# Seven block products for eight over eighteen down-projection blocks in two stages, with p1 first

## The chip, the cores and the metric

The kernel runs on one core of one Trainium2 chip. The metric is device time in microseconds (us) of one execution. The kernel before takes 1212.17 us, the median of three runs (1211.62 to 1212.28).

## The reference, cut to what matters

Two layers (`DEPTH` 2) on 512 tokens (`S`) of width 1024. Each layer is an attention part (retention and stick-breaking heads sharing one input and one output projection) and a SwiGLU feed-forward part with an inner width of 2816, all in float32:

```
h = rms_norm(x, norm2_g[l])
x = x + (jax.nn.silu(h @ w_gate[l]) * (h @ w_up[l])) @ w_down[l]
```

The change touches only the product with `w_down`. The inner width is 22 blocks of 128. For two of these blocks, an even and an odd one, the product is a sum of 2 by 2 blocks: two token halves of 256, two inner blocks of 128, two output halves of 512. Such a product can be had with seven block products in place of eight, from sums and differences of the blocks (Strassen's scheme).

## The kernel before, in words

Every float32 operand is split into a high and a low part, and each product is three matmuls: high by high, high by low, low by high (`mm3`). The high part is a cast on ScalarE (ACT), the low part a subtraction on VectorE (DVE). TensorE (PE) runs its matmuls in the order in which the program is written; the instructions of the other engines are put in order ahead of time by a scheduler, which orders them by priority and estimated time. Each engine, and the queue of loads on SyncE (SP), then works in that order.

Weights come as a stream (`WeightStream`): units of 1024 columns are loaded by SP into four raw buffers, and split by ACT (`whi`) and DVE (`wlo`) into three buffers. A unit is used by 24 matmuls of 512 columns; the split of a unit goes into the buffer of the one three places ahead of it, once PE is done with that.

The feed-forward part of a layer (`ffn`) runs on PE as follows. For each of the 22 blocks f: a gate product and an up product of 24 matmuls each, into two banks out of three (`acc`). DVE multiplies both by the token scale (`g`, `u`), ACT applies silu, DVE multiplies `u` by `g`. For f below 10 (`HALVES[0]`), `paired` then forms what the seven products need of the activations: `a11`, and, when the odd block is there, the split of `u` and of two tiles of differences (the tiles `f`, split into `fhi` and `flo`). `f75` serves the products r7 and q5, `f63` serves q6 and q3. At f=4, 5 and 6 the blocks of `w_down` are asked for (`load_pair`, L732 to L735, tiles `q`, 256 KB each), and DVE adds the first two of each pair (L735); the scheduler is free to put loads and sums earlier.

After f=9 comes the stage of seven products (`down_seven`), for five pairs: q5, p1, q3, q6, r7, p2, q4, each a sum over the five pairs into one group of PSUM banks. The `w_down` operands of the products are made by DVE from the loaded blocks (`summed`), and split like the weights. In layer 0 a pair takes 7 x 4 x 3 = 84 matmuls of 256 columns, where the plain product takes 2 x 8 x 3 = 48 matmuls of 512 columns. In layer 1 a pair takes 7 x 2 x 3 = 42 matmuls of 512 columns. The results are added to the residual by DVE; q5, p1 and q6 are copied by ACT first.

Then gate and up of f=10 to 21, with the activations split into `ahi` and `alo`, and the rest: the plain product with `w_down` over these twelve blocks, 288 matmuls in each layer. In layer 0 it goes by output blocks d (8 of them); after each, DVE adds the bank to `x[d]`, and `feed` prepares the next layer's input: `hhi` (ACT), `hlo` (DVE), the square (ACT) and the sum of squares `ssq` (GpSimd, POOL). In layer 1 it goes by token blocks, and the final norm follows.

Of the kernel before, what the change touches and what calls it, by code (L numbers as in the profile page):

```python
# [18 lines left out]
P = 128  # L19
DM = 1024  # L20
S = 512
L = 2
# [5 lines left out]
FT = DFF // P  # L28
# [24 lines left out]

SEVEN = ("q5", "p1", "q3", "q6", "r7", "p2", "q4")
PAIRS = 5
HALVES = range(2 * PAIRS), range(2 * PAIRS, FT)
TH = S // 2

SLOTS = 26
# [5 lines left out]
def block_plan():  # L67

    plan = []

    def cols(name, l, col):
        return [(name, l, k, col, P) for k in range(KT)]

    for l in range(L):
        plan += [("w_in", l, k, SV, 512) for k in range(KT)]
        for h in range(NH):
            for c in (SQ, SK, RG):
                plan += cols("w_in", l, c + h * HD)
        plan += [("w_in", l, k, RV, 512) for k in range(KT)]
        for h in range(NH):  # L80
            plan += cols("w_in", l, RQ + h * HD) + cols("w_in", l, RK + h * HD)
        for ds, ks in OUT:
            plan += [("w_out", l, k, d * P, P) for d in ds for k in ks]
        for k in range(KT):
            for f in range(2):
                plan += [("w_gate", l, k, f * P, P), ("w_up", l, k, f * P, P)]
        for half, fs in enumerate(HALVES):
            for f in fs:
                if f >= 2:
                    plan += cols("w_gate", l, f * P) + cols("w_up", l, f * P)  # L90
            if half == 0:
                plan += [("seven", l, p, i, 512) for p in SEVEN for i in range(PAIRS)]
            elif l < L - 1:
                for d in range(KT):
                    plan += [("w_down", l, f, d * P, P) for f in fs]
            else:
                for dh in range(2):
                    plan += [("w_down", l, f, dh * 512, 512) for f in fs]
    return plan
# [138 lines left out]
def layers(ctx, tc, xg_in, xT_in, ws_in, wd_in, gfin_in, cos_in, sin_in, dec_in, out):  # L238
    nc = tc.nc
# [9 lines left out]
    pe = Stream(nc)  # L249
    wst = WeightStream(nc, wpool, rawpool, ws_in)  # L250
# [29 lines left out]
    for k in range(KT):  # L280
# [23 lines left out]
        out=mask16, in_=mask16, compare_op=ALU.is_gt, fill=-BIG,  # L304
# [405 lines left out]
    def ffn(l):  # L710
        last = l == L - 1
        with tc.tile_pool(name=f"ff{l}", bufs=1, reuse_waits="tile") as sb:
# [11 lines left out]

            b11, b12, b22, b21 = {}, {}, {}, {}

            def load_block(to, i, n, odd, dh):
                to[i] = block(n)
                nc.sync.dma_start(out=to[i], in_=wd_in[l, 2 * i + odd, :, dh * 512 : dh * 512 + 512])

            def load_pair(i):
                load_block(b12, i, i, 0, 1)  # L732
                load_block(b11, i, PAIRS + i, 0, 0)
                load_block(b22, i, 2 * PAIRS + i, 1, 1)
                nc.vector.tensor_tensor(out=b12[i], in0=b12[i], in1=b11[i], op=ALU.add)  # L735

            def summed(p, i):

                if p == "q6":
                    nc.vector.tensor_tensor(out=b12[i], in0=b12[i], in1=b22[i], op=ALU.add)  # L740
                    load_block(b21, i, 2 * PAIRS + i, 1, 0)
                elif p == "r7":
                    nc.vector.tensor_tensor(out=b11[i], in0=b12[i], in1=b11[i], op=ALU.subtract)
                elif p == "q4":
                    nc.vector.tensor_tensor(out=b12[i], in0=b12[i], in1=b21[i], op=ALU.add)
                src = {"p1": b11, "r7": b11, "p2": b21, "q3": b22}.get(p, b12)
                return src[i]
# [37 lines left out]
            def gated(f, pg, pu):  # L785
                g = sb.tile([P, S], F32, tag="g", name="g", bufs=2)
                nc.vector.tensor_tensor(out=g, in0=pg, in1=rs, op=ALU.mult)  # L787
                act(out=g, in_=g, func=AF.Silu)
                u = sb.tile([P, S], F32, tag="u", name="u", bufs=3)
                nc.vector.tensor_tensor(out=u, in0=pu, in1=rs, op=ALU.mult)  # L790
                nc.vector.tensor_tensor(out=u, in0=u, in1=g, op=ALU.mult)  # L791
                if f in HALVES[0]:
                    return paired(f, u)
                n = 2 * (f - HALVES[1][0])
                hi, lo = slot(n, "ahi"), slot(n + 1, "alo")
                split(hi, lo, u)
                acts[f] = hi, lo

            even, fac = {}, {p: [] for p in SEVEN}
            t0, t1 = slice(0, TH), slice(TH, S)  # L800

            def paired(f, u):


                def home(n, name):
                    n += f // 2 * 7
                    if n < SLOTS:
                        return slot(n, name)
                    return sb.tile([P, S], F32R, tag=f"more{n}", name=name, bufs=1)

                def both(n, src, p, q):
                    hi, lo = home(n, "fhi"), home(n + 1, "flo")
                    split(hi, lo, src)
                    fac[p].append((hi[:, t0], lo[:, t0]))
                    fac[q].append((hi[:, t1], lo[:, t1]))

                def minus(out, a, b):
                    nc.vector.tensor_tensor(out=out, in0=a, in1=b, op=ALU.subtract)
# [12 lines left out]
                both(0, f75, "r7", "q5")  # L831
                minus(f63[:, t0], v[:, t0], f75[:, t1])
                minus(f63[:, t1], u[:, t0], f63[:, t0])
                both(2, f63, "q6", "q3")

            def down_seven():
                n = 2 if last else 4
                w = 512 if last else TH

                def part(t, dh, j):  # L840
                    if last:
                        return xtd[2 * t + j][:, dh * 512 : dh * 512 + 512]
                    return x[4 * dh + j][:, t * TH : t * TH + TH]
# [2 lines left out]

                def evac(p, ps, j):
                    def put(t, dh, op):
                        y = part(t, dh, j)
# [19 lines left out]

                for m, p in enumerate(SEVEN):  # L870
                    if last:
                        pss = [bank() if m % 3 == 2 else bank("z", 4) for _ in range(n)]
                    else:
                        pss = banks_b() if m % 2 else banks_a()
                    for i in range(PAIRS):
                        b = wst.block("seven", l, p, i, 512)
                        a = fac[p][i]
                        for j in range(n):
                            c = slice(j * P, j * P + P)
                            if last:  # L880
                                pe.mm3(pss[j], [v[:, c] for v in a], b, i == 0, i == PAIRS - 1)
                            else:
                                pe.mm3(
                                    pss[j][:, :TH], [v[:, c] for v in b], a,
                                    i == 0, i == PAIRS - 1,
                                )
                    for j in range(n):
                        evac(p, pss[j][:, :w], j)

                def to(t, dh, j, src, op=ALU.add):  # L890
                    y = part(t, dh, j)
# [24 lines left out]
                for tb in range(TB):  # L916
                    pe.later(8000 + 4000 * tb, lambda tb=tb: turn(tb))

            for half, fs in enumerate(HALVES):
                if half == 1 and last:  # L920
                    gfin = [block(KT + i) for i in range(2)]
                    for dh in range(2):
                        nc.sync.dma_start(out=gfin[dh], in_=gfin_in[:, dh * 512 : dh * 512 + 512])
                for f in fs:
                    if f < 2:
                        continue
                    for i in {4: (0, 1), 5: (2, 3), 6: (4,)}.get(f, ()):
                        load_pair(i)
                    pg, pu = bank(), bank()
                    for ps, name in ((pg, "w_gate"), (pu, "w_up")):  # L930
                        for k in range(KT):
                            w = wst.block(name, l, k, f * P, P)
                            pe.mm3(ps, w, (hhi[k], hlo[k]), k == 0, k == KT - 1)
                    gated(f, pg, pu)
                if half == 0:
                    down_seven()
                    continue
                if not last:
                    table_set(EXP_LN)
# [97 lines left out]
```

## Time and profile before

| | |
|---|---|
| median of three runs | 1212.17 us |
| the profiled execution | 1213.44 us |
| its span | 1211.7 us |
| PE busy | 1197.0 us (99%) |
| DVE busy | 750.4 us (62%) |
| ACT busy | 533.4 us (44%) |
| POOL busy | 149.3 us (12%) |

The span is the time from the first to the last record of the profile; the execution is 1.74 us longer. A busy share is an average over all stages; the view by stretches shows the stages apart. The time of a matmul in the records (about 0.39 us for 512 columns) overlaps with the next one's, so the pace of PE is read from the distance between starts.

### The profile page before, as it was taken

Reading aid. Unit: us, or ns where it says so; the run is one execution under the profiler, and the core shown is the slowest. Engines: PE = TensorE matmul, PEld = TensorE weight load, DVE = VectorE, ACT = ScalarE, POOL = GpSimd, SP = SyncE. Lnnn points to the kernel's source line nnn. Section 1 sums busy time; section 2 is a strip of 40 time slices with the busy share of each in tenths; the row PEclk is TensorE's granted clock in tenths of the full one; section 3 lists DMA queues with packets and bytes.
Section 4 is the critical chain, followed back from the end, with each engine's and each line's share of the span. In section 5 each row is a group of like instructions: output and inputs, shape, how many; then the busy total and the mean of one; then the engine's idle time right before and its main releaser. Section 6 shows DMA issues by size and latency. Waiting matters only on the chain.

```text
span 1211.7 us, 14527 instructions
## 1 busy us (share of the span) xinstructions
PE 1197.0 (99%) x5624; PEld 995.5 (82%) x5624; DVE 750.4 (62%) x1048; ACT 533.4 (44%) x812; POOL 149.3 (12%) x135
## 2 busy tenths in 40 slices
PE   9999999999999999999999999999999999999997
PEld 7888887878889988888888888878888788888886
DVE  7566788696568744444344668887865785444333
ACT  6467645453335332333334766444533442332323
POOL 1122054030000000001112212432200000000011
PEclk9999999999999999999999999999999999999999
DMA  7322222353211233233332222224342113232321
GB/s 261 105 70 70 87 89 70 102 202 97 94 53 44 70 105 96 95 99 110 104 105 87 70 70 85 90 70 140 115 139 102 35 62 104 87 104 89 103 70 70
DMA packets 36790, 115.79 MB, mean 96 GB/s; under 512 B 4081, under 2 KB 4081, under 8 KB 36721
## 3 DMA queue, kind: packets, MB, share of 16 engines
q1 hardware_dynamic: 36576, 114.60, 28.1%
q8 instruction: 44, 0.72, 0.2%
q10 hardware_dynamic: 144, 0.26, 0.1%
q14 instruction: 26, 0.20, 0.1%
HBM read 112.75 MB, written 2.10 MB: 95 GB/s over the span
## 4 chain that ended last, share of the span: by engine, by line
PE 91%; DVE 4%; POOL 2%; issue 1%; ACT 1%; DMA 1%; SPq 0%; POOLq 0%; ACTq 0%; DVEq 0%
PE acc L217 69%; PE z L217 17%; PE o L217 4%; PE z L228 1%; POOL k L475 1%; POOL slo L326 1%; POOL qlo L326 1%; DVE wlo L159 0%; ACT whi L157 0%; DMA q<-wd 0%; POOL q L475 0%; DVE p L626 0%; DVE wlo L152 0%; DMA wraw<-ws 0%; DVE m L635 0%
## 5 line engine op out<-in xcount | busy, mean ns | idle before, releaser
L217 PE MATMUL acc<-hhi,whi 128*128 128x512 f32 x960 | 376.0, 392 | 0.0
L217 PE MATMUL acc<-hhi,wlo 128*128 128x512 f32 x960 | 374.1, 390 | 0.0
L217 PE MATMUL acc<-hlo,whi 128*128 128x512 f32 x960 | 373.8, 389 | 0.0
L157 ACT CAST whi<-wraw 128x1024 fp32r<-128x1024 f32 (+1 forms) x185 | 193.2, 1044 | 350.7 <-PE acc L217 161.1
L159 DVE TENSOR_TENSOR wlo<-wraw,whi 128x1024 fp32r<-128x1024 f32 (+1 forms) x185 | 233.2, 1261 | 98.1 <-ACT whi L157 97.4
L217 PEld LDWEIGHTS acc<-hhi,wlo 128*128 128x128 f32 x960 | 180.2, 188 | 38.0
L217 PEld LDWEIGHTS acc<-hhi,whi 128*128 128x128 f32 x960 | 180.3, 188 | 36.3
L217 PEld LDWEIGHTS acc<-hlo,whi 128*128 128x128 f32 x960 | 180.3, 188 | 36.2
L790 DVE TENSOR_TENSOR u<-acc,rs 128x512 f32<-128x512 f32 x40 | 27.6, 691 | 121.0 <-PE acc L217 121.0
L343 POOL TENSOR_TENSOR ssq<-ssq,sqx 128x512 f32<-128x512 f32 x21 | 32.4, 1543 | 386.6 <-ACT sqx L342 386.3
L787 DVE TENSOR_TENSOR g<-acc,rs 128x512 f32<-128x512 f32 x40 | 27.6, 691 | 71.7 <-PE acc L217 71.7
L151 ACT CAST whi<-q 128x512 fp32r<-128x512 f32 x70 | 40.1, 619 | 56.6 <-PE acc L217 28.4
L967 POOL TENSOR_TENSOR xtd<-xtd,q 128x512 f32<-128x512 f32 x7 | 9.2, 1315 | 339.3 <-ACT fsq L963 339.3
L152 DVE TENSOR_TENSOR wlo<-q,whi 128x512 fp32r<-128x512 f32 x70 | 46.1, 684 | 7.2 <-ACT whi L151 7.2
L217 PE MATMUL acc<-mhi,whi 128*128 128x512 f32 x112 | 44.4, 396 | 1.7 <-DVE x L679 1.7
L217 PE MATMUL acc<-mlo,whi 128*128 128x512 f32 x112 | 44.2, 394 | 0.1
L217 PE MATMUL acc<-mhi,wlo 128*128 128x512 f32 x112 | 44.0, 393 | 0.0
L217 PE MATMUL acc<-ahi,whi 128*128 128x512 f32 x96 | 37.3, 389 | 0.0
L217 PE MATMUL acc<-alo,whi 128*128 128x512 f32 x96 | 37.3, 389 | 0.0
L217 PE MATMUL acc<-ahi,wlo 128*128 128x512 f32 x96 | 37.3, 389 | 0.0
L326 POOL TENSOR_TENSOR slo<-sq,shi 128x512 fp32r<-128x512 f32 x16 | 23.6, 1475 | 83.9 <-ACT shi L325 83.9
L791 DVE TENSOR_TENSOR u<-u,g 128x512 f32<-128x512 f32 x44 | 30.4, 690 | 3.4
(281 smaller groups left out, 2065.5 us busy)
## 6 DMA issues: line engine op xcount, KB each, us to landing
wraw<-ws SPq DMA_DIRECT2D x183, 512.0 KB, 3.5
q<-wd SPq DMA_DIRECT2D x40, 256.0 KB, 5.3
dec<-dec SPq DMA_DIRECT2D x8, 256.0 KB, 3.2
x<-xT SPq DMA_DIRECT2D x7, 256.0 KB, 6.2
out<-q SPq DMA_DIRECT2D x7, 256.0 KB, 2.0
wraw<-ws SPq DMA_DIRECT2D x2, 256.0 KB, 4.3
cosrs<-cos SPq DMA_DIRECT2D x2, 256.0 KB, 4.5
sinrs<-sin SPq DMA_DIRECT2D x2, 256.0 KB, 4.7
```

The lines of the kernel that those rows point to most:

```text
L151: copy = nc.scalar.copy(out=hi[:, c], in_=src)
L152: nc.vector.tensor_tensor(out=lo[:, c], in0=src, in1=hi[:, c].bitcast(F32), op=ALU.subtract)
L157: copy = nc.scalar.copy(out=hi[:, c], in_=raw[:, c])
L159: nc.vector.tensor_tensor(out=lo[:, c], in0=raw[:, c], in1=hi[:, c].bitcast(F32), op=ALU.subtract)
L217: self.nc.tensor.matmul(ps, lhsT=lhsT, rhs=rhs, start=start, stop=stop)
L228: self.nc.tensor.transpose(out, src, ident)
L326: eng.tensor_tensor(out=lo, in0=src, in1=hi.bitcast(F32), op=ALU.subtract)
L343: eng.tensor_tensor(out=ssq, in0=ssq, in1=q, op=ALU.add)
L475: nc.gpsimd.tensor_tensor(out=r, in0=t1, in1=t2, op=ALU.add)
L787: nc.vector.tensor_tensor(out=g, in0=pg, in1=rs, op=ALU.mult)
L790: nc.vector.tensor_tensor(out=u, in0=pu, in1=rs, op=ALU.mult)
L791: nc.vector.tensor_tensor(out=u, in0=u, in1=g, op=ALU.mult)
```

## The change

The first 18 of the 22 blocks are now done by seven products, in two stages: five pairs after f=9 (as before), four pairs after f=17. The rest has four blocks, f=18 to 21, 96 matmuls in each layer. The list of products begins with p1, which needs `a11` of the activations and a loaded block as it is, and q5 comes second. The loads of a pair's blocks are held behind the last weight load written before them (`issue_after`).

```
-SEVEN = ("q5", "p1", "q3", "q6", "r7", "p2", "q4")
-PAIRS = 5
-HALVES = range(2 * PAIRS), range(2 * PAIRS, FT)
+SEVEN = ("p1", "q5", "q3", "q6", "r7", "p2", "q4")
+PAIRS = (5, 4)
+STARTS = (0, 10, 18)
+PARTS = [range(a, b) for a, b in zip(STARTS, STARTS[1:] + (FT,))]
+REST = PARTS[-1]
...
-            def load_pair(i):
-                load_block(b12, i, i, 0, 1)
-                load_block(b11, i, PAIRS + i, 0, 0)
-                load_block(b22, i, 2 * PAIRS + i, 1, 1)
+            def load_pair(part, i):
+                with tc.issue_after(wst.loads[-1]):
+                    load_block(b12, part, i, i, 0, 1)
+                    load_block(b11, part, i, PAIRS[0] + i, 0, 0)
+                    load_block(b22, part, i, 2 * PAIRS[0] + i, 1, 1)
                 nc.vector.tensor_tensor(out=b12[i], in0=b12[i], in1=b11[i], op=ALU.add)
...
-                if f in HALVES[0]:
+                if f not in REST:
                     return paired(f, u)
...
-                    for i in range(PAIRS):
-                        b = wst.block("seven", l, p, i, 512)
+                    for i in range(pairs):
+                        b = wst.block("seven", l, (part, p), i, 512)
...
-                    for i in {4: (0, 1), 5: (2, 3), 6: (4,)}.get(f, ()):
-                        load_pair(i)
+                    for i in {4: (0, 1), 5: (2, 3), 6: (4,)}.get(f - fs[0], ()):
+                        if fs is not REST and i < PAIRS[part]:
+                            load_pair(part, i)
...
-                if half == 0:
-                    down_seven()
+                if fs is not REST:
+                    down_seven(part)
                     continue
```

The buffers of the first stage (blocks `q`, activation slots, kept copies) serve the second again.

Three places show what moves. The first is DVE's queue at the end of the output projection of layer 0, where the residual is updated ahead of the feed-forward part. Before:

```order
L329 SCALAR_TENSOR_TENSOR hlo_136<-x_85,xg,hhi_128 128x512
L735 TENSOR_TENSOR q<-q 128x512
L679 TENSOR_TENSOR x_88<-x_88,acc 128x512
L159 TENSOR_TENSOR wlo_2256<-wraw_2206,whi_2255 128x1024
L679 TENSOR_TENSOR x_89<-x_89,acc 128x512
```

Now, at the same place:

```order
L331 SCALAR_TENSOR_TENSOR hlo_136<-x_85,xg,hhi_128 128x512
L681 TENSOR_TENSOR x_88<-x_88,acc 128x512
L161 TENSOR_TENSOR wlo_2256<-wraw_2206,whi_2255 128x1024
L681 TENSOR_TENSOR x_89<-x_89,acc 128x512
L331 SCALAR_TENSOR_TENSOR hlo_137<-x_86,xg,hhi_129 128x512
```

The sum of two loaded blocks (`q<-q`) stood between two steps of the residual; all five of them are gone from here and stand behind the first gate and up products.

The second is DVE's queue at the start of a stage of seven products in layer 0, from the last `u` to the split of `f75` (`flo<-f`). Before, in the one stage:

```order
L791 TENSOR_TENSOR u<-u,g 128x512
L152 TENSOR_TENSOR wlo_3154<-q,whi_3153 128x512
L740 TENSOR_TENSOR q<-q 128x512
L818 TENSOR_TENSOR f<-u 128x256
L743 TENSOR_TENSOR q<-q 128x512
L326 TENSOR_TENSOR flo<-u,fhi 128x512
L152 TENSOR_TENSOR wlo_3184<-q,whi_3183 128x512
L818 TENSOR_TENSOR f<-u,f 128x256
L152 TENSOR_TENSOR wlo_3184<-q,whi_3183 128x512
L326 TENSOR_TENSOR flo<-f,fhi 128x512
```

Now, in the second stage:

```order
L796 TENSOR_TENSOR u<-u,g 128x512
L154 TENSOR_TENSOR wlo_4447<-q,whi_4446 128x512
L745 TENSOR_TENSOR q<-q 128x512
L826 TENSOR_TENSOR f<-u 128x256
L745 TENSOR_TENSOR q<-q 128x512
L328 TENSOR_TENSOR flo<-u,fhi 128x512
L748 TENSOR_TENSOR q<-q 128x512
L154 TENSOR_TENSOR wlo_4477<-q,whi_4476 128x512
L826 TENSOR_TENSOR f<-u,f 128x256
L154 TENSOR_TENSOR wlo_4477<-q,whi_4476 128x512
L748 TENSOR_TENSOR q<-q 128x512
L328 TENSOR_TENSOR flo<-f,fhi 128x512
```

The split of `f75` is no nearer to the front of the queue; it stands two instructions further back.

The third is PE's order at the start of the rest in layer 0, its first bank (numbers name the buffers; each `ahi` is one block f, `alo` the next number). Before, these six are the last of the 36 matmuls of that bank, for f=20 and f=21:

```order
L217 MATMUL acc_4653<-ahi_4576,whi99_4612 128x512
L217 MATMUL acc_4653<-alo_4577,whi99_4612 128x512
L217 MATMUL acc_4653<-ahi_4576,wlo99_4613 128x512
L217 MATMUL acc_4653<-ahi_4648,whi99_4612 128x512
L217 MATMUL acc_4653<-alo_4649,whi99_4612 128x512
L217 MATMUL acc_4653<-ahi_4648,wlo99_4613 128x512
```

Now the whole first bank, f=18 to f=21:

```order
L219 MATMUL acc_5259<-ahi_5038,whi112_5188 128x512
L219 MATMUL acc_5259<-alo_5039,whi112_5188 128x512
L219 MATMUL acc_5259<-ahi_5038,wlo112_5189 128x512
L219 MATMUL acc_5259<-ahi_5110,whi112_5188 128x512
L219 MATMUL acc_5259<-alo_5111,whi112_5188 128x512
L219 MATMUL acc_5259<-ahi_5110,wlo112_5189 128x512
L219 MATMUL acc_5259<-ahi_5182,whi112_5188 128x512
L219 MATMUL acc_5259<-alo_5183,whi112_5188 128x512
L219 MATMUL acc_5259<-ahi_5182,wlo112_5189 128x512
L219 MATMUL acc_5259<-ahi_5254,whi112_5188 128x512
L219 MATMUL acc_5259<-alo_5255,whi112_5188 128x512
L219 MATMUL acc_5259<-ahi_5254,wlo112_5189 128x512
```

Block f=21, whose activations are made last, is used after nine matmuls, where it was used after thirty-three.

## Rows read from the trace of the kernel before

**Rows 1.** The page: busy by engine, granted clock, chain that ended last, loads.

```profile
PE 1197.0 (99%) x5624; PEld 995.5 (82%) x5624; DVE 750.4 (62%) x1048; ACT 533.4 (44%) x812; POOL 149.3 (12%) x135
...
PEclk9999999999999999999999999999999999999999
...
PE 91%; DVE 4%; POOL 2%; issue 1%; ACT 1%; DMA 1%; SPq 0%; POOLq 0%; ACTq 0%; DVEq 0%
...
q<-wd SPq DMA_DIRECT2D x40, 256.0 KB, 5.3
```

**Rows 2.** Stretches: seven products of layer 0 and 1, rest of layer 0 and 1.

```profile
core 0: us, PE busy (x) PEld busy (x) DVE busy (x) ACT busy (x) POOL busy (x), PEclk, DMA share, GB/s
357.99:409.54 51.55, 50.55 (x421) 50.34 (x420) 44.02 (x86) 25.31 (x48) 0.00 (x0) 1.00 0.10 31
958.62:1007.95 49.33, 48.38 (x211) 39.32 (x210) 42.72 (x70) 24.72 (x42) 0.00 (x0) 1.00 0.13 41
540.14:605.42 65.28, 65.28 (x289) 54.05 (x288) 26.41 (x29) 22.91 (x28) 9.29 (x6) 1.00 0.31 105
1138.51:1203.79 65.28, 65.28 (x289) 53.87 (x287) 22.23 (x31) 19.47 (x32) 8.83 (x7) 1.00 0.17 57
```

**Rows 3.** Timeline of PE, seven products: start, time, what, [idle before, releaser].

```profile
363.74 0.28 PE L217 MATMUL z<-fhi,whi 128*128 128x256 f32 x1
365.02 0.39 PE L217 MATMUL z<-flo,whi 128*128 128x256 f32 x1 [1.00 <-DVE flo L326]
...
964.30 0.40 PE L217 MATMUL z<-wlo,fhi 128*128 128x512 f32 x1
965.65 0.50 PE L217 MATMUL z<-whi,flo 128*128 128x512 f32 x1 [0.95 <-DVE flo L326]
```

**Rows 4.** Timeline of DVE at the same place of layer 0.

```profile
364.28 0.68 DVE L326 TENSOR_TENSOR flo<-f,fhi 128x512 fp32r<-128x512 f32 x1
364.89 0.68 DVE L743 TENSOR_TENSOR q<-q 128x512 f32<-128x512 f32 x1
```

**Rows 5.** Timeline of PE, output projection of layer 0.

```profile
245.09 0.39 PE L217 MATMUL acc<-mhi,wlo 128*128 128x512 f32 x1
247.17 0.50 PE L217 MATMUL acc<-mhi,whi 128*128 128x512 f32 x1 [1.70 <-DVE x L679]
```

**Rows 6.** Timeline of DVE at the same place.

```profile
244.83 1.69 DVE L735 TENSOR_TENSOR q<-q 128x512 f32<-128x512 f32 x1 [0.45 <-DMA q<-wd]
...
246.44 0.68 DVE L679 TENSOR_TENSOR x<-x,acc 128x512 f32<-128x512 f32 x1
```

**Rows 7.** Timeline of DVE and POOL, output projection of layer 1.

```profile
841.62 1.79 DVE L329 SCALAR_TENSOR_TENSOR hlo<-x,xg,hhi 128x512 fp32r<-128x512 f32 x1
...
843.71 3.53 POOL L343 TENSOR_TENSOR ssq<-ssq,sqx 128x512 f32<-128x512 f32 x2 [0.85 <-ACT sqx L342]
843.93 2.16 DVE L159 TENSOR_TENSOR wlo<-wraw,whi 128x1024 fp32r<-128x1024 f32 x1
```

**Rows 8.** Timeline, start of the rest in layer 0: PE, then DVE, then ACT.

```profile
540.14 0.39 PE L217 MATMUL acc<-ahi,whi 128*128 128x512 f32 x1
...
541.75 1.22 DVE L159 TENSOR_TENSOR wlo<-wraw,whi 128x1024 fp32r<-128x1024 f32 x1
542.88 0.69 DVE L326 TENSOR_TENSOR alo<-u,ahi 128x512 fp32r<-128x512 f32 x1
...
541.87 0.62 ACT L325 CAST ahi<-u 128x512 fp32r<-128x512 f32 x1 [0.65 <-DVE u L791]
```

**Rows 9.** The same in layer 1: PE, then DVE.

```profile
1138.51 0.39 PE L217 MATMUL acc<-whi,ahi 128*128 128x512 f32 x1
...
1141.25 0.69 DVE L326 TENSOR_TENSOR alo<-u,ahi 128x512 fp32r<-128x512 f32 x1
```

**Rows 10.** Timeline of DVE in the rest of layer 0, late.

```profile
598.95 0.75 DVE L329 SCALAR_TENSOR_TENSOR hlo<-x,xg,hhi 128x512 fp32r<-128x512 f32 x1 [0.79 <-ACT hhi L328]
```

**Rows 11.** Timeline of DVE, gate and up of layer 1, sum of loaded blocks.

```profile
894.37 0.69 DVE L735 TENSOR_TENSOR q<-q 128x512 f32<-128x512 f32 x1 [5.06 <-DMA q<-wd]
```

More of the change, by code (lines that the diff above doesn't have):

```diff
@@ L86, in block_plan @@
                 plan += [("w_gate", l, k, f * P, P), ("w_up", l, k, f * P, P)]
-        for half, fs in enumerate(HALVES):
+        for n, fs in enumerate(PARTS):
             for f in fs:
@@ L90, in block_plan @@
                     plan += cols("w_gate", l, f * P) + cols("w_up", l, f * P)
-            if half == 0:
-                plan += [("seven", l, p, i, 512) for p in SEVEN for i in range(PAIRS)]
+            if fs is not REST:
+                plan += [("seven", l, (n, p), i, 512) for p in SEVEN for i in range(PAIRS[n])]
             elif l < L - 1:
@@ L725, in ffn, with load_block, summed @@
             b11, b12, b22, b21 = {}, {}, {}, {}
-            def load_block(to, i, n, odd, dh):
+            def load_block(to, part, i, n, odd, dh):
                 to[i] = block(n)
-                nc.sync.dma_start(out=to[i], in_=wd_in[l, 2 * i + odd, :, dh * 512 : dh * 512 + 512])
-            def load_pair(i):
-                load_block(b12, i, i, 0, 1)
-                load_block(b11, i, PAIRS + i, 0, 0)
-                load_block(b22, i, 2 * PAIRS + i, 1, 1)
+                f = STARTS[part] + 2 * i + odd
+                nc.sync.dma_start(out=to[i], in_=wd_in[l, f, :, dh * 512 : dh * 512 + 512])
+            def load_pair(part, i):
[3 more added lines that the diff above has]
+                    load_block(b22, part, i, 2 * PAIRS[0] + i, 1, 1)
                 nc.vector.tensor_tensor(out=b12[i], in0=b12[i], in1=b11[i], op=ALU.add)
-            def summed(p, i):
+            def summed(key, i):
+                part, p = key
                 if p == "q6":
                     nc.vector.tensor_tensor(out=b12[i], in0=b12[i], in1=b22[i], op=ALU.add)
-                    load_block(b21, i, 2 * PAIRS + i, 1, 0)
+                    load_block(b21, part, i, 2 * PAIRS[0] + i, 1, 0)
                 elif p == "r7":
@@ L791, in gated @@
                 nc.vector.tensor_tensor(out=u, in0=u, in1=g, op=ALU.mult)
-                if f in HALVES[0]:
+                if f not in REST:
                     return paired(f, u)
-                n = 2 * (f - HALVES[1][0])
+                n = 2 * (f - REST[0])
                 hi, lo = slot(n, "ahi"), slot(n + 1, "alo")
@@ L797, in gated @@
                 acts[f] = hi, lo
-            even, fac = {}, {p: [] for p in SEVEN}
+            even, fac = {}, {}
             t0, t1 = slice(0, TH), slice(TH, S)
             def paired(f, u):
+                at = max(n for n in STARTS if n <= f)
+                if f == at:
+                    fac.update({p: [] for p in SEVEN})
                 def home(n, name):
-                    n += f // 2 * 7
+                    n += (f - at) // 2 * 7
                     if n < SLOTS:
@@ L834, in paired, with down_seven, place @@
                 both(2, f63, "q6", "q3")
-            def down_seven():
+            def down_seven(part):
+                pairs = PAIRS[part]
                 n = 2 if last else 4
                 w = 512 if last else TH
-                def part(t, dh, j):
+                def place(t, dh, j):
                     if last:
@@ L848, in put @@
                     def put(t, dh, op):
-                        y = part(t, dh, j)
+                        y = place(t, dh, j)
                         nc.vector.tensor_tensor(out=y, in0=y, in1=ps, op=op)
@@ L880, in down_seven @@
                             if last:
-                                pe.mm3(pss[j], [v[:, c] for v in a], b, i == 0, i == PAIRS - 1)
+                                pe.mm3(pss[j], [v[:, c] for v in a], b, i == 0, i == pairs - 1)
                             else:
@@ L884, in down_seven @@
                                     pss[j][:, :TH], [v[:, c] for v in b], a,
-                                    i == 0, i == PAIRS - 1,
+                                    i == 0, i == pairs - 1,
                                 )
@@ L890, in to @@
                 def to(t, dh, j, src, op=ALU.add):
-                    y = part(t, dh, j)
+                    y = place(t, dh, j)
                     nc.vector.tensor_tensor(out=y, in0=y, in1=src, op=op)
@@ L917, in ffn @@
                     pe.later(8000 + 4000 * tb, lambda tb=tb: turn(tb))
-            for half, fs in enumerate(HALVES):
-                if half == 1 and last:
+            for part, fs in enumerate(PARTS):
+                if fs is REST and last:
                     gfin = [block(KT + i) for i in range(2)]
@@ L934, in ffn @@
                     gated(f, pg, pu)
-                if half == 0:
-                    down_seven()
+                if fs is not REST:
+                    down_seven(part)
                     continue
@@ L1015 @@
             at += w
-    wd = np.ascontiguousarray(a["w_down"][:, : 2 * PAIRS * P].reshape(L, 2 * PAIRS, P, DM))
+    wd = np.ascontiguousarray(a["w_down"][:, : REST[0] * P].reshape(L, REST[0], P, DM))
     cols = []
```

## Prediction

> **What bounds the kernel now.** I read the page first: PE is busy 99% of the span and the chain that ended last is 91% PE, at a granted clock of full speed in every slice, that is 2.4 GHz [rows 1]. The reader should see that no other engine is near its limit over the whole, so time is won only by taking matmuls away or by closing gaps between them. Then the stretches, for the price of a matmul where the change works. In the rest of layer 0, 288 matmuls of 512 columns take 65.28 us: 0.2267 us each, with nothing between them; in layer 1 the same [rows 2]. The stage of seven products takes 51.55 us for 420 matmuls of 256 columns in layer 0, and 49.33 us for 210 of 512 in layer 1 [rows 2]. Then the timeline of PE for gaps over a microsecond. Three matter here: 363.74 to 365.02, where the step would be 0.12, so 1.16 us lost, and 964.30 to 965.65, where it would be 0.23, so 1.12 lost, both in the first product (q5), waiting for the low part of a difference tile (flo) of the last pair [rows 3]; and 245.09 to 247.17 in the output projection of layer 0, 1.85 lost, waiting for a residual update of DVE [rows 5]. Last, what DVE did before those: the update came late since a sum of loaded blocks stood ahead of it, which waited 0.45 us for its load and then took 1.69 us, where its like takes 0.69 [rows 6, 11].
>
> **Fewer matmuls.** Without its gap the stage of layer 0 is 50.39 us for 420 matmuls, 0.120 each: the pace of 256 columns is more than half of 0.2267, and TensorE's weight loads are busy 50.34 us there, so they fill the stage [rows 2]. A pair costs 84 x 0.120 = 10.08 us and the two plain blocks that it replaces 48 x 0.2267 = 10.88: 0.80 saved. In layer 1 a pair is 42 x (49.33 - 1.12) / 210 = 9.64 us, 1.24 saved [rows 2]. Four more pairs in each layer: 3.2 + 5.0 = 8.2 us.
>
> **p1 first.** Its activations (`a11`) come from the even block and are there long before; its loaded block needs no sum. q5 follows after 60 matmuls in the first stage and 48 in the second. The last pair's flo, which ended 364.28 + 0.68 - 357.99 = 6.97 us after the stage began [rows 2, 4], is wanted in layer 0 after 48 + 36 = 84 x 0.12 = 10.1 us in the second stage, and after 13.0 in the first. The order puts two more sums ahead of it, each 0.61 by the distance of two starts [rows 4]: 8.2. In layer 1 it is wanted after 42 x 0.23 = 9.6. So it is in time by 1.4 us or more at all four starts: the two gaps go, 1.16 + 1.12 = 2.3 us, and the two new stages bring none. If the margin were gone, each of the four starts would cost about 1.14.
>
> **Loads behind the weights.** The five sums leave the place between the residual updates in layer 0. Without them DVE stands as it did in layer 1, where the weight split next to the same step takes 2.16 us beside POOL's sums [rows 7] and PE shows no gap of that kind. I take the whole 1.85 us; the bounds are 0 (the split of 2.16 us takes the sum's place as the late one) and 1.85. What is late next is the sums' own wait: they now stand between `g` and `u` of the first blocks of each part, and hold DVE until their loads land, 5.3 us after issue in the median [rows 1]. Such a wait is in the trace, in layer 1: 5.06 us of idle DVE, with `u` and a weight split queued behind, and PE has no gap there [rows 11]. The cover is the lead of the splits: the split that begins when a unit ends is done 541.75 + 1.22 - 540.14 = 2.83 us later [rows 8] and wanted two units on, 2 x 24 x 0.2267 = 10.88 us, so 8.05 us of lead. I cost the waits at nothing.
>
> **The rest starts with four blocks.** This is new and on the path. The activations of the last block are ready 541.87 + 0.62 - 540.14 = 2.35 us (high) and 542.88 + 0.69 - 540.14 = 3.43 us (low) after the last gate-and-up matmul [rows 8]; DVE's order there is as before. PE used the last block after 33 matmuls, 7.5 us; now after 9, 2.04 us. In layer 0 the low part is wanted by its second matmul, at 2.27: a gap of 1.16, with 0.06 from end to start as in [rows 3, 4], 1.2 us. In layer 1 it is wanted by the third, at 2.49; it was there at 1141.25 + 0.69 - 1138.51 = 3.43 [rows 9], and the matmul after such a gap is late by another 0.1: 1.1 us. Together -2.3. Bounds: 0, if the gap is taken up elsewhere, and 4.6, if the weight split in front of it doubles as it did beside POOL [rows 7].
>
> **DVE in the second stage.** The first stage holds 44.02 us of DVE in layer 0 and 42.72 in layer 1 [rows 2]. One pair fewer takes away 7 low splits and 3 sums at 0.61, 6.1 us; what comes per stage (taking up the results, the end of the last block's chain) stays. That leaves 37.9 us in 40.3 in layer 0 and 36.6 in 38.6 in layer 1: 94 and 95%, where the first stage has 85 and 87. I take no gap from it, since the splits keep ahead by up to two units; the bounds are 0 and what it would be if DVE needed the same idle time as in the first stage, 37.9 + 7.5 - 40.3 = 5.1 and 36.6 + 6.6 - 38.6 = 4.6.
>
> **DVE in the rest of layer 0.** The feeds of the next layer come every 2.72 us (12 matmuls) and no more every 8.16. For two of them DVE needs two updates of 0.68 [rows 6], two `hlo` of 0.75 [rows 10] and one weight split of 1.22 [rows 8], 4.1 us of 5.44; beside POOL, `hlo` took 1.79 and the split 2.16 [rows 7], and with these it is 7.1. I take 0.3 us, near the lower end, since `hlo` in this very stage takes 0.75 [rows 10].
>
> The Trainium skill speaks against the change here: by its page SBUF — State Buffer (on the shared port pair) a DVE operation with two SBUF inputs and a GpSimd operation that reads SBUF hold one pair of ports in turn, each for its whole length. The trace agrees, with 0.75 for `hlo` alone and 1.79 in the stretch where POOL sums. By the rule, with feeds three times as close, the longer times would be the usual ones; that result is rival B below, worked out from rows.
>
> **The sum.** 8.2 + 2.3 + 1.85 - 2.3 - 0.3 = 9.7 us. The profiled execution, 1213.44 us with 1.74 around its span of 1211.7, would come to 1203.7; it is 1.27 above the median of the runs shown, so against the median: 1212.17 - 9.7 = 1202.5 us.
>
> **The rivals.**
> A. DVE bounds the second stages. For it: 94 and 95%. Against: the first stage, with the same work at its start and its end, lost only the flo gap [rows 3], which p1 now covers. Half of the bounds above, 4.8 us: 1207.3; all of them, 9.7, and nothing is won: 1212.2.
> B. DVE and POOL stand in each other's way in the rest of layer 0. At 7.1 us for 5.44, DVE falls back by 1.66 for each two blocks, 6.6 us in all. Three `acc` banks let PE run two blocks ahead, 5.4 us, so at least 1.2 reaches PE and at most 6.6: 1203.4 to 1208.8, or 1206 in the middle. For it: 1.79 and 2.16 in [rows 7]. Against: 0.75 in [rows 10].
> C. The change does not do what it says: p1 first only moves the gap, or the output projection keeps its own. Four gaps for two is 2 x 2.3 = 4.6 more: 1207.1; only the output projection: 1204.4.
> D. Slower: the sums of loaded blocks hold DVE at each of the first two or three blocks of a part, and the waits add up. Three of 5.06 us are 15.2, less the lead of 8.05, 7.1 us for PE in each of four places: 28.5 us, 1231. It decides from the point where DVE is late by more than the lead at two blocks in a row. For it: [rows 11], and that all loads now stand behind weight loads. Against: it takes several such waits in a row, and the trace has one that reached PE nowhere; a load lands in 5.3 us [rows 1], less than a block's 10.88.
>
> **How the numbers follow.** The forecast, 1200.5 to 1204.5, has 0.60; A 0.13 (most of it near the half, 0.03 near all), B 0.13, C 0.10, D 0.04. The lower end of the range is the sum without the gap at the rest and without crowding, 1212.17 - 12.35 = 1199.8, set to 1199.5; the upper end takes in B's middle and nearly half of A and C, 1207. What is left out is the full A, D and the ends of B and C, under 2 in 10. A change of under 0.2% (2.4 us) can't be told from none. All cases but the full A and D are faster by more than that: faster 0.92, same 0.04, slower 0.04.
>
> **What would show it.** Stages of 50.4 and 40.3 us in layer 0, 48.2 and 38.6 in layer 1, PE without gaps over 0.5 us in them; no gap by 245 us; at both starts of the rest one gap of about 1.1 us that names the low activation part; feeds in the rest of layer 0 with `hlo` near 0.75. Wrong would be: gaps of PE in the second stages that name `wlo` or `flo`; a rest of layer 0 much longer than 21.8 + 1.2 us; PE waiting for weight splits behind `q<-q`.

## The result and the profile after

The kernel after takes 1203.72 us (median of 4 runs, 1203.63 to 1204.16) beside 1211.89 of the kernel before (4 runs): a ratio of 0.9933, 95% interval 0.9916 to 0.9951. The forecast was 1202.5, the range 1199.5 to 1207.0.

The page of the kernel after, its profiled execution with a span of 1202.0 us and a time of 1204.16. The lines answer to [rows 1].

```profile
PE 1189.2 (99%) x5744; PEld 995.0 (83%) x5744; DVE 829.1 (69%) x1230; ACT 562.1 (47%) x886; POOL 150.8 (13%) x135
...
PEclk9999999999999999999999999999999999999999
...
PE 94%; DVE 2%; POOL 1%; issue 1%; ACT 1%; DMA 0%; SPq 0%; DVEq 0%; ACTq 0%; POOLq 0%
...
L739 DVE TENSOR_TENSOR q<-q 128x512 f32<-128x512 f32 x18 | 12.4, 691 | 28.8 <-DMA q<-wd 28.8
...
q<-wd SPq DMA_DIRECT2D x72, 256.0 KB, 4.9
```

PE is still busy 99% of the span at a clock of full speed; it has 7.8 us less to do, and DVE 79 us more. The 18 sums of loaded blocks (L739, in the kernel before L735) sat waiting for their loads for 28.8 us in all.

The stretches of the kernel after: first stage of seven products, second stage and rest of layer 0, then the same of layer 1 (columns as in [rows 2]).

```profile
356.48:406.78 50.30, 50.30 (x422) 50.30 (x420) 46.00 (x90) 25.14 (x48) 0.00 (x0) 1.00 0.10 33
493.86:534.11 40.25, 40.25 (x337) 40.24 (x336) 39.15 (x76) 21.09 (x41) 0.00 (x0) 1.00 0.09 30
577.64:600.75 23.11, 22.32 (x97) 17.94 (x96) 16.44 (x21) 14.54 (x21) 8.43 (x6) 1.00 0.34 115
953.96:1002.09 48.13, 48.13 (x212) 39.39 (x210) 44.70 (x74) 24.63 (x42) 0.00 (x0) 1.00 0.11 36
1089.13:1127.34 38.21, 38.21 (x169) 31.53 (x168) 38.01 (x63) 20.70 (x35) 0.00 (x0) 1.00 0.12 38
1170.86:1193.94 23.08, 22.53 (x97) 17.60 (x95) 12.68 (x23) 11.08 (x24) 8.91 (x7) 1.00 0.07 24
```

In the four stages of seven products PE's busy time is the stretch itself: they have no gap, where each of the two in [rows 2] had one of a microsecond. DVE is busy 39.15 of 40.25 us and 38.01 of 38.21 in the second stages, 97 and 99%. Of the six stretches only the two rests have idle PE.

PE at the start of the rest of layer 0, then of layer 1, kernel after:

```profile
579.46 0.39 PE L219 MATMUL acc<-ahi,wlo 128*128 128x512 f32 x1
580.04 0.49 PE L219 MATMUL acc<-ahi,whi 128*128 128x512 f32 x1 [0.19 <-ACT ahi L327]
581.12 0.50 PE L219 MATMUL acc<-alo,whi 128*128 128x512 f32 x1 [0.59 <-DVE alo L328]
...
1172.67 0.39 PE L219 MATMUL acc<-whi,alo 128*128 128x512 f32 x1
1173.26 0.50 PE L219 MATMUL acc<-whi,ahi 128*128 128x512 f32 x1 [0.20 <-ACT ahi L327]
1173.59 0.40 PE L219 MATMUL acc<-wlo,ahi 128*128 128x512 f32 x1
1174.34 0.50 PE L219 MATMUL acc<-whi,alo 128*128 128x512 f32 x1 [0.35 <-DVE alo L328]
```

Starts of two matmuls lie 0.23 apart without a wait, so 0.35 + 0.85 = 1.2 us are lost in layer 0 and 0.36 + 0.10 + 0.52 = 1.0 in layer 1. The smaller wait is for the high part of the last block, the larger for its low part.

### The profile page after: what moved, and what is told of

The parts are those of the page before. It is cut to its first block, busy times and chain, and to the rows that moved or that the text cites. A ratio compares the mean times of both kernels' runs of the same rounds, so it can differ in the third digit from the quotient of the medians.

```text
span 1202.0 us, 15062 instructions
## 1 busy us (share of the span) xinstructions
PE 1189.2 (99%) x5744; PEld 995.0 (83%) x5744; DVE 829.1 (69%) x1230; ACT 562.1 (47%) x886; POOL 150.8 (13%) x135
## 4 chain that ended last, share of the span: by engine, by line
PE 94%; DVE 2%; POOL 1%; issue 1%; ACT 1%; DMA 0%; SPq 0%; DVEq 0%; ACTq 0%; POOLq 0%
PE acc L219 68%; PE z L219 21%; PE o L219 4%; PE z L230 1%; DVE wlo L161 1%; DMA x<-xT 0%; POOL k L477 0%; POOL slo L328 0%; POOL qlo L328 0%; POOL q L477 0%; DVE p L628 0%; DVE ptlo L328 0%; ACT whi L159 0%; PE ps_rst L219 0%; DVE m L637 0%
## 5 line engine op out<-in xcount | busy, mean ns | idle before, releaser
L159 ACT CAST whi<-wraw 128x1024 fp32r<-128x1024 f32 (+1 forms) x169 | 176.4, 1044 | 254.6 <-PE acc L219 117.1
L161 DVE TENSOR_TENSOR wlo<-wraw,whi 128x1024 fp32r<-128x1024 f32 (+1 forms) x169 | 215.2, 1274 | 51.4 <-ACT whi L159 50.2
L153 ACT CAST whi<-q 128x512 fp32r<-128x512 f32 x126 | 72.1, 620 | 97.9 <-PE acc L219 31.1
L154 DVE TENSOR_TENSOR wlo<-q,whi 128x512 fp32r<-128x512 f32 x126 | 83.1, 686 | 1.9 <-ACT whi L153 1.9
L327 ACT CAST fhi<-f 128x512 fp32r<-128x512 f32 x36 | 22.4, 622 | 26.7 <-DVE f L826 26.7
L739 DVE TENSOR_TENSOR q<-q 128x512 f32<-128x512 f32 x18 | 12.4, 691 | 28.8 <-DMA q<-wd 28.8
L219 PE MATMUL z<-wlo,hhi 128*128 128x512 f32 x80 | 31.5, 394 | 0.5 <-DVE wlo L161 0.5
```

The source lines that it names most:

```text
L153: copy = nc.scalar.copy(out=hi[:, c], in_=src)
L154: nc.vector.tensor_tensor(out=lo[:, c], in0=src, in1=hi[:, c].bitcast(F32), op=ALU.subtract)
L159: copy = nc.scalar.copy(out=hi[:, c], in_=raw[:, c])
L161: nc.vector.tensor_tensor(out=lo[:, c], in0=raw[:, c], in1=hi[:, c].bitcast(F32), op=ALU.subtract)
L219: self.nc.tensor.matmul(ps, lhsT=lhsT, rhs=rhs, start=start, stop=stop)
L327: nc.scalar.copy(out=hi, in_=src)
```

## The experiments

**Theory P** is the prediction: matmuls taken away, two `flo` gaps and the gap at 245 us closed, a new gap at each rest. The **rivals** are A (DVE bounds the second stages), B (DVE and POOL hold each other up in the rest of layer 0), C (order or loads do nothing) and D (waits of the sums reach PE).

**The kernel before, a second profiled execution** (`before_again`), no edit.

> The kernel before, unchanged, profiled once more. The trace of the change shows TensorE's work between the first weight product and the last matmul 10.55 us shorter than before, but the medians differ by 8.2 us only. Theory P (that execution of before was a slow one of its kind): the new profile shows a shorter gap at 245 us in the output projection, or an earlier start, and its span is nearer to 1210.5 than to 1211.7. Theory Q (the difference lies outside of TensorE's work, at the start and the end of an execution): the gap at 245 us is 1.85 us again, the stages are as before to 0.1 us, and only the first 25 us and what follows the last matmul differ.

1211.87 us (1211.5 to 1213.49), ratio 0.9999 (0.999 to 1.0007). The place of [rows 5, 6] in this second execution: DVE, POOL, then PE.

```profile
244.46 0.69 DVE L735 TENSOR_TENSOR q<-q 128x512 f32<-128x512 f32 x1
245.07 0.68 DVE L679 TENSOR_TENSOR x<-x,acc 128x512 f32<-128x512 f32 x1
...
244.71 5.52 POOL L343 TENSOR_TENSOR ssq<-ssq,sqx 128x512 f32<-128x512 f32 x3 [0.84 <-ACT sqx L342]
...
245.09 0.39 PE L217 MATMUL acc<-mhi,wlo 128*128 128x512 f32 x1
245.80 0.50 PE L217 MATMUL acc<-mhi,whi 128*128 128x512 f32 x1 [0.32 <-DVE x L679]
```

The load was there, the sum took 0.69 us where it had taken 1.69, and PE lost 0.48 where it had lost 1.85. The two executions differ in which engine came first. POOL's row in the first one:

```profile
244.69 2.96 POOL L343 TENSOR_TENSOR ssq<-ssq,sqx 128x512 f32<-128x512 f32 x2 [0.86 <-ACT sqx L342]
```

There DVE's sum started at 244.83, after it; here at 244.46, ahead of POOL's 244.71. So the 1.85 us were those of one execution. The stages are as in the first one: 51.55, 65.28 and 49.35 us.

The times fall in two groups that fit this. Of the 47 executions of the kernel before that were timed with `before_again` and `hold_only`, 34 lie between 1211.44 and 1212.49 us, 13 between 1213.02 and 1213.54, and none between the groups. The first profiled execution, with a gap of 1.85, took 1213.44; this one, with 0.48, took 1212.07: 1.37 less in the time and 1.37 less in the gap. No other execution of this kernel was profiled, so that all 13 had the long gap is likely and not shown.

**The loads' hold taken back** (`loads_free`):

```diff
-                with tc.issue_after(wst.loads[-1]):
-                    load_block(b12, part, i, i, 0, 1)
...
+                load_block(b12, part, i, i, 0, 1)
...
```

> The changed kernel without the hold on the loads of down blocks. Theory (the sums in front of the residual updates cost the gap at 245 us): the gap of some 1.85 us is back in the output projection of layer 0, and the time is 1.5 to 2.1 us above the changed kernel, about 1205.5. Rival (the gap came from other work of VectorE and GpSimd and the hold is worth nothing): no gap there, 1203.7 within 0.5. A second rival: loads of the second part, now issued early, get in the way of weights, and TensorE waits for weight splits near 410 us.

1203.98 us (1203.23 to 1207.99), ratio 0.9939 (0.9925 to 0.9952): 0.3 us above the kernel after, and the expectation of 1.5 to 2.1 missed. PE loses 0.67 us at this place, with DVE's sum at 244.57 ahead of POOL's at 244.64 and 0.69 long; every stage is as in the kernel after.

**The hold alone, in the kernel before** (`hold_only`), the same lines the other way round.

> The kernel before with one part of the change alone: each pair's three loads of down blocks and its sum wait for the weight load issued last; the order of products and the 20 paired blocks are as before. Theory P as predicted (the gap of 1.85 us at 245 us goes): 1.85 us less, 1210.2. Theory P with the term re-sized (a second profiled execution of the kernel before has 0.48 us there and the kernel after without this part 0.67): 0.3 to 0.7 us less, 1211.3 to 1211.7. Rival (without the sums between the residual updates nothing is gained, since the loads that come later cost elsewhere): no change or slower, 1212.1 and more.

1211.73 us beside 1211.93, ratio 0.9996 (0.9987 to 1.0004). The gap at 245 us is gone; the two `flo` gaps stand, 1.16 and 1.12 us. DVE at the place:

```profile
244.27 0.67 DVE L679 TENSOR_TENSOR x<-x,acc 128x512 f32<-128x512 f32 x1
244.87 2.16 DVE L159 TENSOR_TENSOR wlo<-wraw,whi 128x1024 fp32r<-128x1024 f32 x1
```

The split that now stands there takes 2.16 us, as in [rows 7], and PE has no gap behind it. What this part is worth lies between the 0.2 us of the medians here and the 0.5 to 0.7 of gaps in the two traces above. The interval of the ratio takes in no change. The means differ by 0.5 us, 1211.71 against 1212.22: none of these 11 executions is above 1212.05, where 4 of the 15 beside them are in the upper group.

**p1 first alone, in the kernel before** (`p1_only`):

```diff
-SEVEN = ("q5", "p1", "q3", "q6", "r7", "p2", "q4")
+SEVEN = ("p1", "q5", "q3", "q6", "r7", "p2", "q4")
```

> The kernel before with one line changed: p1 the first of the seven products, q5 the second; still 20 of 44 down blocks in pairs, loads as they were. Theory P (the prediction's step, priced by the two gaps of 1.16 and 1.12 us in the kernel before): both gaps for the low part of a difference tile go, and nothing else changes: 2.3 us less, about 1209.6. Rival (the order is worth more than the gaps, as the run with the old order and 18 paired blocks per layer could suggest, where it was worth 9.9 us): 5 us or more less, under 1207. Rival (the gap only moves to another product): no change, 1211.9.

1209.74 us beside 1212.12, ratio 0.9984 (0.9975 to 0.9992): 2.4 us less for 2.3 expected. The stages take 50.31 and 48.13 us. The half of rival C that is about the order falls here, the other half with `hold_only`.

**The old order, in the kernel after** (`q5_first`), the same line the other way round.

> The changed kernel with the products in the old order, q5 ahead of p1. Theory (the last pair's difference tile is some 7 us behind the start of a stage and q5 wants it too soon): gaps of about 1.15 us in the first stage of each layer as before, and in the second stages, where q5 reaches the last pair after three pairs and no more four, larger ones: 7.0 - 4.3 = 2.7 us in layer 0 and 7.0 - 4.1 = 2.9 in layer 1. Sum 7.9 us, time about 1211.5. Rival (the weight splits ahead of the stage are the bound and the order of products is nothing): within 1 us of 1203.7. In between: the same 1.15 in all four, 4.6 us, 1208.3.

1213.85 us, ratio 1.001 (1.0001 to 1.0019), 2.3 above the expected 1211.5: without p1 first the other parts win nothing. PE in the second stage of layer 0, which began at 494.97:

```profile
499.17 0.28 PE L219 MATMUL z<-fhi,wlo 128*128 128x256 f32 x1
499.69 0.38 PE L219 MATMUL z<-fhi,whi 128*128 128x256 f32 x1 [0.24 <-ACT fhi L327]
502.01 0.39 PE L219 MATMUL z<-flo,whi 128*128 128x256 f32 x1 [1.94 <-DVE flo L328]
```

The last pair's `flo` is there 502.01 - 494.97 = 7.0 us after the start, as it was in the first stage [rows 4]. But with three pairs ahead of it and not four, q5 asks for it after 36 matmuls, 4.3 us. So a second stage loses more than the 1.14 us by which the prediction priced it: in layer 0 it takes 42.95 us against 40.25, 2.70 more. In layer 1 it takes 42.46 against 38.21, 4.25 more, and there the waits are only a part. PE's two waits, then a stretch behind them (columns as in [rows 2]):

```profile
1099.06 0.50 PE L219 MATMUL z<-whi,fhi 128*128 128x512 f32 x1 [0.73 <-ACT fhi L327]
...
1101.13 0.50 PE L219 MATMUL z<-whi,flo 128*128 128x512 f32 x1 [1.33 <-DVE flo L328]
...
1101.64:1105.06 3.42, 3.42 (x9) 2.66 (x9) 2.76 (x6) 2.73 (x5) 0.00 (x0) 0.50 0.00 0
```

From 1101.64 to 1105.06 the granted clock was 0.50 of full speed, 1.2 GHz and not 2.4, and matmuls started 0.43 apart and not 0.23. That is some 1.7 of the 4.25 us; the waits are the other 2.6, where 2.9 was expected. In layer 0 waits of 0.24 and 1.94 brought no such fall. With 1.26 and 1.17 in the first stages the four stages lose 9.4 us: 7.7 by waits, where 7.9 was expected and four times 1.14 would be 4.6, and 1.7 by the clock. The other executions point the same way: the five with a mean granted clock of 0.997 take 1212.56 to 1213.33 us, the six with 0.995 or 0.996 take 1213.85 to 1214.83.

**More work for DVE** (`dve_plus8`, and `dve_plus24` with 6 in place of 2), in the kernel after:

```diff
                 if p == "q6":
                     nc.vector.tensor_tensor(out=b12[i], in0=b12[i], in1=b22[i], op=ALU.add)
+                    for _ in range(2 if part else 0):
+                        more = sb.tile([P, TH], F32, tag="more", name="more", bufs=1)
+                        b = b12[i]
+                        nc.vector.tensor_tensor(out=more, in0=b[:, :TH], in1=b[:, TH:], op=ALU.add)
```

> The kernel after with eight additions of 256 columns more on DVE in the second stage of each layer, two for each pair, behind the sum for q6, into a tile that nothing reads; about 0.33 us each, so 2.7 us of DVE per second stage. Theory P (DVE's 94 and 95 per cent in the second stages bound nothing, since its operands are ready ahead): what is idle there, 40.3 - 37.9 = 2.4 us in layer 0 and 2.0 in layer 1, takes most of it up: the time stays within 1 us of the kernel after, 1203.7 to 1204.7. Rival A (DVE bounds the second stages): every added microsecond comes out, 2 x 2.7 = 5.4 us: 1209.

> The same with 24 such additions in the second stage of each layer, six for each pair: 8.0 us of DVE per second stage, more than is idle there. Theory P: the idle 2.4 and 2.0 us take up their part, and the splits' lead a little more, so at most 5.6 + 6.0 = 11.6 us come out and probably about half of it: 1207 to 1215. Rival A: all 16 us come out: 1220.

1209.38 us (ratio 0.9978, 0.9968 to 0.9987) and 1229.12 (1.0142, 1.0128 to 1.0156): 5.7 and 25.4 us more than the kernel after. The second stages of `dve_plus8`, layers 0 and 1:

```profile
493.76:534.37 40.61, 40.52 (x338) 40.30 (x336) 40.41 (x83) 21.27 (x41) 0.00 (x0) 1.00 0.09 27
1089.36:1132.64 43.28, 39.58 (x170) 32.02 (x168) 42.55 (x74) 20.59 (x35) 0.00 (x0) 0.98 0.16 54
```

PE's longest wait in the second of them, from the timeline:

```profile
1126.65 0.50 PE L219 MATMUL z<-whi,fhi 128*128 128x512 f32 x1 [0.30 <-ACT whi L153]
1130.56 0.58 PE L219 MATMUL z<-wlo,fhi 128*128 128x512 f32 x1 [3.41 <-DVE wlo L154]
```

Layer 0 hid nearly all of its 2.7 us (0.36 lost, none of it in a gap over 0.3). Layer 1 paid 5.07 us in the stage and 0.8 behind it, more than was added. The total is near the one that rival A expected, the way is not: nearly all came from one layer, and it has two parts that are not DVE's added time.

The first is the scheduler's: with the additions it put the last pair's sum and split behind residual updates and weight splits, and the split ran at 1129.82, where it was over at 1122.9 in the kernel after. The second is the clock, which fell right behind the wait:

```profile
1129.82 0.68 DVE L154 TENSOR_TENSOR wlo<-q,whi 128x512 fp32r<-128x512 f32 x1
...
1130.83:1134.24 3.41, 3.41 (x9) 2.65 (x9) 2.85 (x5) 1.05 (x1) 0.00 (x0) 0.50 0.45 163
```

The waits come to 4.1 us. The matmuls at half the clock come to 1.7: 0.9 in the stage and the 0.8 behind it. So the runs don't price a microsecond of DVE, nor do they show how much layer 1 had to spare.

The larger dose is above both expectations. Its three stretches at half the clock, one in layer 0 and two in layer 1:

```profile
532.20:545.85 13.65, 9.41 (x36) 8.28 (x37) 11.98 (x26) 3.75 (x5) 0.00 (x0) 0.50 0.23 78
1139.77:1143.19 3.42, 3.22 (x6) 1.75 (x6) 3.28 (x9) 0.34 (x1) 0.00 (x0) 0.50 0.00 0
1150.01:1153.43 3.42, 3.42 (x10) 2.64 (x9) 2.79 (x5) 1.05 (x1) 0.00 (x0) 0.50 0.09 37
```

PE is busy 9.41 + 3.22 + 3.42 = 16.05 us in them. Half of that, 8 us, is an estimate of what the clock cost. The other 17 of the 25.4 us are near the 16 that rival A expected. That fits DVE as the bound at this dose; what a moved order of instructions adds here too, no run separates.

**The last block of the rest used later** (`late_last`). In layer 0 the first three of the eight output blocks take three blocks f first and the fourth behind them (the plan of weights likewise); in the first half of layer 1 three blocks run for all token tiles and the last one behind them:

```diff
+                    for d in range(3):
+                        rest(pss[d], d, fs[:-1])
+                    for d in range(3):
+                        rest(pss[d], d, fs[-1:])
+                    for d in range(3, KT):
+                        rest(bank(), d, fs)
...
-                    tail = 4
+                    tail = 4 if dh else 1
```

> The changed kernel, but the rest uses the last block (f=21) later: in layer 0 three banks take f=18 to 20 first and f=21 after 27 matmuls, in layer 1 the first output half takes f=21 after 36. Theory (the gaps at the starts of the rest, 1.2 and 0.9 us in the trace of the change, are the wait for the last block's activations and nothing else): both gaps go, time about 2.1 us lower, 1201.6. Rival (VectorE or the weight splits are late there anyway and the gap moves to the next bank): 0 to 1 us lower, with gaps in the first banks of the rest that name other tiles.

1201.44 us (1201.08 to 1201.56), ratio 0.9909 (0.9896 to 0.9923): 2.3 us under the kernel after, and the best of all. The two rests:

```profile
577.08:599.24 22.16, 22.06 (x98) 17.94 (x96) 17.27 (x19) 12.99 (x18) 7.66 (x5) 1.00 0.30 97
1169.34:1191.27 21.93, 21.92 (x97) 17.84 (x95) 12.70 (x23) 11.11 (x24) 8.76 (x7) 1.00 0.07 26
```

Beside 23.11 and 23.08 above they are shorter by 0.95 and 1.15: the gaps at the start of the rest were waits for the last block, and the order could have avoided them.

**One pair more** (`ten_pairs`), on top of `late_last`:

```diff
-PAIRS = (5, 4)
-STARTS = (0, 10, 18)
+PAIRS = (5, 5)
+STARTS = (0, 10, 20)
```

> The kernel with the last block of the rest used later (late_last), with one more pair: 20 of the 22 down blocks of each layer in two stages of five pairs, and a rest of two blocks. In the rest of layer 0 a step of 8 blocks then ends every 6 matmuls, 1.36 us, not every 2.72, so DVE's update, high part and split (0.68 + 0.75 + 0.6 = 2.0 us) are asked for faster than DVE gives them. Theory P for matmuls alone: one pair more saves 0.8 us in layer 0 and 1.24 in layer 1, 2.0 in all, and the shorter rest costs a new gap of about 1.2 us in layer 0 and 0.7 in layer 1: no change against late_last, 1201.4. Rival B (DVE and POOL set the pace of the rest of layer 0): 8 feeds at 2.0 us and more are late by 5 us and more behind 8 x 1.36, of which the first queries and keys of layer 1 feel 2 to 5: 1203.5 to 1206.5.

1207.78 us, ratio 0.9963 (0.9951 to 0.9976), 6.3 more than `late_last`, above both expectations. The second stages have no gap. Layer 0 loses 1.05 us from its first stage to the end of its rest (244.37 us against 243.32), since the gap of 1.2 is back and a wait for a residual update adds 0.75; rival B wanted 2 to 5 for such waits. The stretched `hlo` of rival B is there, with feeds every 1.36 us: it took 1.78 us at 600.31, behind a sum of POOL from 600.09. Layer 1 wins 0.87 on PE (237.96 against 238.83, from its first stage to the last matmul). The rest of the loss comes after PE's end. Last matmul and the last two of the four token scales of the final norm, `ten_pairs`, then `late_last`:

```profile
1190.94 0.39 PE L219 MATMUL z<-whi,alo 128*128 128x512 f32 x1
...
1198.33 0.16 DVE L361 SCALAR_TENSOR_TENSOR frn<-u,r 128x1 f32<-128x1 f32 x1
...
1200.01 0.16 DVE L361 SCALAR_TENSOR_TENSOR frn<-u,r 128x1 f32<-128x1 f32 x1
```

```profile
1190.88 0.39 PE L219 MATMUL z<-whi,alo 128*128 128x512 f32 x1
...
1192.47 0.16 DVE L361 SCALAR_TENSOR_TENSOR frn<-u,r 128x1 f32<-128x1 f32 x1
1194.30 0.16 DVE L361 SCALAR_TENSOR_TENSOR frn<-u,r 128x1 f32<-128x1 f32 x1
```

PE ends at the same moment, the last scale comes 5.7 us later: with two blocks a token tile ends every 1.36 us, and the scales follow one another in 1.7 to 2.3. The end has become a chain of DVE, ACT and POOL.

**The kernel after, once more** (`after_again`), no edit.

> The kernel after once more, on the same chip as the run beside it, for a second look at its places: stages of 50.3, 40.25, 48.1 and 38.2 us without a gap over 0.5, gaps of 1.2 and 0.9 us at the two starts of the rest, and at 245 us none; 1203.7. If the gaps at the rest come from the order alone, they are there again to 0.1 us; if from chance as at 245 us, they are not.

1203.28 us, ratio 0.9927 (0.9913 to 0.994); stages of 50.31, 40.25, 48.14 and 38.21 us, losses of 1.2 and 1.0 us at the starts of the rests, none at 245 us.

## Why the prediction was right, and the one term that was not

The second profiled executions of both kernels, `before_again` and `after_again`, have spans of 1210.3 and 1201.1 us: 9.2 between them. By places of PE: first stages 51.55 - 50.31 = 1.24 and 49.35 - 48.14 = 1.21; output projection 17.86 - 17.25 = 0.61; the rest of layer 0 against second stage and rest 65.28 - 40.25 - 23.08 = 1.95; in layer 1, to the start of the last matmul, 65.05 - 38.21 - 22.73 = 4.11. Together 9.1. The times differ by less: an execution of the kernel before is 1.8 us longer than its span (1212.07 and 1210.3), one of the kernel after 2.2 (1203.28 and 1201.1, 1204.16 and 1202.0). The prediction carried these 0.4 us as unchanged, and no run shows where they come from.

- **Fewer matmuls**, 3.2 + 5.0. Layer 0: 1.95 with the new gap of 1.2 added is 3.15; layer 1: 4.11 + 1.0 = 5.1. Right.
- **p1 first**, 2.3. Measured alone 2.4; the first stages win 1.24 and 1.21. In the second stage of layer 0 the last pair's `flo` ends 8.2 us after the start, as worked out, and is wanted after 10.1:

```profile
501.36 0.68 DVE L328 TENSOR_TENSOR flo<-f,fhi 128x512 fp32r<-128x512 f32 x1
```

- **Loads behind the weights**, 1.85. This term was mis-sized: 0.2 to 0.7 in the runs. The step that failed was "I take the whole 1.85 us", from one execution, at the upper of its two bounds. Most of it was an order of two engines that another execution did not have, and the prediction had a sign of it in hand: the execution that it read was 1.27 us above the median. It took these 1.27 off the time at the end and gave them no place. Had it taken them off this gap, 1.85 - 1.27 = 0.58 would have been left. By rows: the sum took 1.69 us when it began 0.14 behind a sum of POOL (244.83 against 244.69), and 0.69 when it began ahead of one, by 0.25, 0.07 and 0.38 us (`before_again`, `loads_free`, `p1_only`). By the Trainium skill's page SBUF — State Buffer (section SBUF: two separate sides) whichever of the two starts first has the shared port pair for its whole instruction, and the other waits; the four rows agree.
- **The rest with four blocks**, -2.3: measured 1.2 + 1.0 = 2.2. `late_last` took both gaps away and won 2.3 in the medians, 0.95 + 1.15 = 2.1 by places.
- **DVE in the second stages**, no gap: right, but the size was not. DVE has 39.15 and 38.01 us there, not 37.9 and 36.6. The prediction counted down from the first stages before, 44.02 and 42.72 us, and these did not stay: they hold 46.00 and 44.70 now. All five sums for q6 stand in them, where four of the five had run ahead of the stage. DVE in the first stage of layer 0, kernel before, then after:

```profile
L740 DVE TENSOR_TENSOR q<-q 128x512 f32<-128x512 f32 x1 | 0.7, 683 | 0.0
...
L745 DVE TENSOR_TENSOR q<-q 128x512 f32<-128x512 f32 x5 | 3.4, 688 | 0.0
```

 Rival A was nearer than 94 and 95% made it look: DVE idled 0.2 us in the second stage of layer 1. How near, no run measures.
- **DVE in the rest of layer 0**, -0.3: 23.08 us less the gap of 1.2 is 21.88, where 96 matmuls at 0.2267 take 21.76, so 0.1 at most. Rival B did not come. DVE and POOL there in `after_again`:

```profile
585.84 0.74 DVE L331 SCALAR_TENSOR_TENSOR hlo<-x,xg,hhi 128x512 fp32r<-128x512 f32 x1
...
585.88 1.85 POOL L345 TENSOR_TENSOR ssq<-ssq,sqx 128x512 f32<-128x512 f32 x1 [329.47 <-ACT sqx L344]
588.63 1.29 POOL L345 TENSOR_TENSOR ssq<-ssq,sqx 128x512 f32<-128x512 f32 x1 [0.90 <-ACT sqx L344]
```

 DVE's `hlo` begins 0.04 ahead of POOL's sum; it keeps its 0.74 us, and POOL's takes 1.85 in place of 1.29. The rule on the port pair holds, but POOL was the one that waited, and PE has no wait for POOL there. That feeds closer still make DVE wait, `ten_pairs` shows.
- **Rival D**: DVE's sums waited 28.8 us for their loads, and PE has no gap in those gate and up products. That the splits' lead covered the waits is the prediction's account; no run varied the lead.

With 0.2 to 0.7 for 1.85 the sum is 8.05 to 8.55, which against the 1212.17 shown is 1203.6 to 1204.1: measured 1203.72 and 1203.28. The forecast's miss of 1.2 us is about this one term. Among the others some 0.5 us more was won than forecast, and 0.4 lost outside the span; that these cancel is luck.

## What to carry to other kernels

Order the first consumer of a stage by what is ready, and count how many instructions of it come before the late operand: a shorter stage asks for that operand sooner, so a gap of one microsecond can double there (1.26 and 2.70 us here). A gap that hangs on which of two engines reaches a shared resource first is worth what several executions show, not what one does; if the profiled execution lies above the median, such a gap is the first place to take the excess from. When an experiment adds work to an engine, read the granted clock and the order of instructions before the price: both moved here. When a stage at the very end is shortened, read the chain behind the last matmul first: it may be the slower one.

## What the runs showed of the hardware

Which of DVE and POOL came first decided who paid, by margins of 0.04 to 0.4 us: `hlo` took 0.74 us beside a POOL sum that it preceded by 0.04, and a sum 1.69 us 0.14 behind one. DVE ran at 99% of a stage of 38.21 us without a gap on PE.

Waits of PE cost more than their length where the granted clock fell to half behind them: to 1.2 GHz, with matmuls of 512 columns 0.43 us apart and not 0.23. It fell behind waits of 0.73 and 1.33 us in `q5_first`, of 3.41 in `dve_plus8`, and of 1.99, 4.92 and 3.23 in `dve_plus24`. It did not behind the 1.70 of [rows 5], nor behind 0.24 and 1.94 in layer 0 of `q5_first`.
